# Output projection of a transformer block: three of the eight pairs of K tiles in its second half as seven products

## The chip, the cores and the metric

The kernel runs on one core of a Trainium2 chip. TensorE (in the profile: PE for its matmuls, PEld for its weight loads) multiplies and writes to PSUM, which has eight banks of 128 x 512 float32. VectorE (DVE) and ScalarE (ACT) do elementwise work, GpSimd (POOL) a few small steps, and SyncE (SP) issues nearly all loads from memory. The metric is the time of one run on the device in microseconds (us), less being better. Each engine takes its instructions in the order in which the program writes them; engines wait for each other through semaphores.

## The reference, cut to what matters

One layer of a hybrid encoder, on 256 tokens of width 2048, all in float32: an input projection, eight heads of retention and eight of latent attention, an output projection, a layer norm, a feed-forward part of width 8192, and a second layer norm.

```python
def reference(x, positions, w_in, ..., w_out, ln1_g, ln1_b, w_up, w_down, ln2_g, ln2_b):
    ...
    mix = jnp.concatenate([ret_out, mla_out], axis=-1) @ w_out[l]      # (256, 2048) @ (2048, 2048)
    x = _layer_norm(DEEPNORM_ALPHA * x + mix, ln1_g[l], ln1_b[l])
    h = jnp.square(jax.nn.relu(x @ w_up[l])) @ w_down[l]
    x = _layer_norm(DEEPNORM_ALPHA * x + h, ln2_g[l], ln2_b[l])
    return x
```

## The kernel before, in words

**Split operands.** Every matmul operand `a` is held as two tiles of TensorE's rounded type: `hi`, a cast by ScalarE, and `lo = a - hi`, a subtraction by VectorE. A product is three matmuls: hi with hi, hi with lo, lo with hi. The activations of the output projection are `mix`: 16 K tiles of 128 rows, each with 256 columns of hi (one per token) and 256 of lo.

**Weights as jobs.** Weights arrive as a list of jobs (`weights`, L174 to L205; `weights_pair` for the feed-forward part). A job has a load of 1 MB into one of three raw tiles (tag `raw`) and pieces that split the raw tile, 1024 columns each: a cast (L190) and a subtraction (L191). The hi and lo tiles come from a ring of five slots (`NSLOT`). `next_piece` (L135) issues the next piece of the list; a piece that needs a slot goes out only if the matmuls of the piece five before it have been issued (`free` marks that). `unit` (L209) is called after each group of matmuls: it advances every generator in the list `side` by one step, and then issues up to two pieces. So side work and weight pieces get their places in the engines' instruction streams by the order of these calls. A job with `held` set stops the list until it is cleared. The last three pairs of the output projection's second half do not use slots: their pieces (`staged_out`) go to tiles of their own, `wsx` and `wst`.

**The output projection** (L821 to L841) computes two halves of 1024 columns. A half is eight steps; each takes a pair of K tiles, `kp = (i + 4) % 8`, so the heads of latent attention come first. For each of the two row blocks `tb` of 128 tokens a step issues 12 matmuls of 128 x 512 (two K tiles, three each, two PSUM banks; `xstat`, L302), and after them a `unit`. A half has four banks, `ao[tb][j]`, of the tag `acc`; the second half reuses those of the first. In the last step of the first half, `residual` (L813) adds each finished bank to the scaled residual stream `xt` (L818) and takes its statistics (L819); block 0's two residuals stand ahead of the `unit` after block 0's matmuls, block 1's ahead of the next.

The second half runs its first five steps in that loop. Its last three, staged, are issued bank by bank (`out_bank`, L916) with the first layer norm between them: `out_bank(0, 0)`, its residual, a `unit`, `out_bank(0, 1)`, its residual, `stats` of block 0, four `n_norm` (L869), five sixths of `out_bank(1, 0)`, and then `n_trans` (L875, tiles `x1t`), the transposes of the first normalised columns, into PSUM banks of the second tag, `wk`. TensorE has this order too.

**Seven products.** The up and down projections of the feed-forward part already do some pairs of K tiles by a Strassen-like scheme (`seven_products`, matmuls at L1090). The pair's weights are a 2 x 2 block matrix, and so are its activations (two K tiles by two row blocks). Seven products instead of eight, 21 matmuls instead of 24, use sums of weight blocks (`weight_sums`, L400 to L402, three VectorE operations) and sums of activation blocks (`token_sums`, L364 to L369). Such a pair has three and a half splits where a plain pair has two. Four of the products collect in four extra banks, which are added to the results afterwards (`add_sums`, L1176, in the down projection).

Of the kernel before, what the change touches and what calls it, by code (L numbers as in the profile page):

```python
# [8 lines left out]
F32 = mybir.dt.float32  # L9
# [5 lines left out]
P = 128  # L15
D = 2048
S = 256
# [22 lines left out]
STORED = (12, 9, 22, 25, 4, 7)  # L40


UP_PAIRS = (3, 5, 6)
UP_SEVEN = ((), (3, 5)) + 6 * (UP_PAIRS,)
NHELD = 4
# [35 lines left out]
def kernel(  # L81
# [35 lines left out]
    def bank(name):  # L117
        return psum.tile([P, 512], F32, tag="wk", name=name)
# [43 lines left out]
    def raw_tile(job, name):  # L162
        job.raw = wraw.tile([P, 2048], F32, tag="raw", name=name)
        return job.raw

    def weights(src, n, name, into=None, width=1024, cuts=None):

        job = Job(None, [], into is None)
        job.width = width
        spans = list(zip(cuts, cuts[1:])) if cuts else [(0, n)]  # L170

        def load():
            raw = raw_tile(job, f"raw_{name}")
            for i, (a, b) in enumerate(spans):  # L174
                (nc.scalar if name == "mla0" and i == 0 else nc.sync).dma_start(raw[:, a:b], src[:, a:b])

        def piece(i):
            a, m = i * width, min(width, n - i * width)
            if into is None:
                hi = wsp.tile([P, 1024], F32R, tag="hi", name=f"hi_{name}_{i}")  # L180
                lo = wsp.tile([P, 1024], F32R, tag="lo", name=f"lo_{name}_{i}")
            else:
                hi, lo = into(i)
            job.hi.append(hi)
            job.lo.append(lo)
            for o, e in spans if cuts else ((a, a + m),):
                o, e = max(o, a) - a, min(e, a + m) - a
                if o < e:
                    r = job.raw[:, a + o:a + e]
                    nc.scalar.copy(hi[:, o:e], r)  # L190
                    nc.vector.tensor_sub(lo[:, o:e], r, hi[:, o:e].bitcast(F32))  # L191

        job.load = load
        job.pieces = [lambda i=i: piece(i) for i in range((n + width - 1) // width)]
        job.free = [[False] for _ in job.pieces]
        jobs.append(job)
        return job

    def other(load, pieces):
        job = Job(None, pieces, False)  # L200
        job.load = lambda: load(job)
        job.free = []
        jobs.append(job)
        return job
# [121 lines left out]
    def staged_out(i):  # L326
        def into(j):
            if i == 0:
                t = work.tile([P, 2048], F32R, tag="big", name=f"wsx{j}", bufs=2)
                return t[:, 0:1024], t[:, 1024:2048]  # L330
            if "out" not in staged:
                staged["out"] = slab.tile([P, 8192], F32R, tag="slab", name="wst")
            o = (2 * i - 2 + j) * 2048
            return staged["out"][:, o:o + 1024], staged["out"][:, o + 1024:o + 2048]
        return into

    for half in range(2):
        row = []
        for i in range(KT // 2):
            kp = (i + H // 2) % (KT // 2)  # L340
            n = i - (KT // 2 - 3)
            row.append(weights(w_out[half, kp], 2048, f"wo{half}{kp}",
                               into=staged_out(n) if half and n >= 0 else None))
        j_out.append(row)
    norm_rows = {}

    def row_job(i, pieces):
        def load(job):
            norm_rows[i] = raw_tile(job, f"row{i}")
            nc.sync.dma_start(norm_rows[i], ln_rows[i:i + 1].partition_broadcast(P))  # L350
        other(load, pieces)

    def x1_piece(i, tb, a):
        c = xt[:, tb, a:a + 1024]
        op = nc.vector.tensor_mul if i == 0 else nc.vector.tensor_add
        op(c, c, norm_rows[i][:, a:a + 1024])


    extra = {}

    def token_sums(r0, r1, st, v):
# [9 lines left out]
    def weights_pair(name, load, half, columns, sums=None, seven=False, into=None):  # L371
# [44 lines left out]
        jobs.append(job)  # L416
        return job

    def up_pair(b, kp):
        def load(job):  # L420
            raw = raw_tile(job, f"raw_wu{b}_{kp}")
            nc.sync.dma_start(raw.rearrange("p (f c) -> p f c", f=8),
                              w_up[8 * b:8 * b + 8, :, kp * 256:(kp + 1) * 256].rearrange("f p c -> p f c"))

        def half(job, e, i, j):
            return job.raw.rearrange("p (f e c) -> p f e c", f=8, e=2)[:, i:j, e]

        def columns(job, t):
            v = job.raw.rearrange("p (f e c) -> p f e c", f=8, e=2)
            return (v[:, 4:8].rearrange("p f e c -> p e f c"), v[:, :, 0].rearrange("p (j f) c -> p j f c", j=2),  # L430
                    t.rearrange("p (j f c) -> p j f c", j=2, c=P))

        return weights_pair(f"wu{b}_{kp}", load, half, columns, None, kp in UP_SEVEN[b])

    def down_pair(p, pair, into=None, seven=None):
# [16 lines left out]
                    job.raw[:, 0:1024].rearrange("p (j c) -> p j c", j=2), t.rearrange("p (j c) -> p j c", j=2))  # L452

        return weights_pair(f"wd{p}_{pair}", load, half, columns, None if seven is None or p == 1 and pair in STORED else sums, seven is not None, into)

    def sums_view(t):
        return t.rearrange("p (i h c) -> p i h c", i=4, h=2)

    def sums_of(q, pair):
        q = 2 + STORED.index(pair) if pair in STORED else q  # L460
# [352 lines left out]
    def residual(tb, j, pb, st, scaled=False):  # L813
# [4 lines left out]
            nc.vector.scalar_tensor_tensor(c, c, ALPHA, pb, op0=ALU.mult, op1=ALU.add)  # L818
        nc.vector.bn_stats(st[:, j], c)  # L819

    def out_steps(half, i):  # L821
        kp = (i + H // 2) % (KT // 2)
        hi, lo = use(j_out[half][i])
        return [(mix, 2 * kp + j, hi, lo, j * 1024) for j in range(2)]

    for half in range(2):
        ao = [[acc(f"o{half}{tb}{j}") for j in range(2)] for tb in range(2)]
        for i in range(KT // 2 - 3 * half):
            if half == 1 and i == 0:
                assert not side  # L830
                work_cm.__exit__(None, None, None)
                work = ctx.enter_context(tc.tile_pool(name="work2", bufs=1))
            steps = out_steps(half, i)
            for tb in range(2):
                xstat(ao[tb], steps, (512, 512), i == 0, half == 0 and i == KT // 2 - 1, tb)
                if half == 0 and i == KT // 2 - 1:
                    for j in range(2):
                        residual(tb, j, ao[tb][j], st1[tb])
                if tb == 1:
                    free(j_out[half][i])  # L840
                unit()  # L841

    mvs, rss = [None] * 2, [None] * 2

# [7 lines left out]
    w_staged = []  # L852
    for i in range(3):
        w_staged += out_steps(1, KT // 2 - 3 + i)
    x1hl = slab.tile([P, KT, 512], F32R, tag="slab", name="x1hl")
    pts = {}


# [58 lines left out]
        xstat(ao[tb], w_staged[part], (512, 512), False, last, tb, banks=(j,))  # L917

    out_bank(0, 0)
    residual(0, 2, ao[0][0], st1[0])  # L920
    unit()
    out_bank(0, 1)
    residual(0, 3, ao[0][1], st1[0])
    stats(0, st1[0])
    unit(1)
    q4 = [range(4 * q, 4 * q + 4) for q in range(4)]
# [7 lines left out]
    n_hi(0, q4[0])  # L934
    n_trans(0, q4[1])
    n_trans(0, q4[2])
    residual(1, 2, ao[1][0], st1[1])
    n_affine(0, q4[1], False)
    n_affine(0, q4[2], True)
    n_lo(0, q4[0])  # L940
# [6 lines left out]
    n_lo(0, q4[2])  # L947
    n_hi(0, q4[3])
    out_bank(1, 1, slice(2, 6), True)
    residual(1, 3, ao[1][1], st1[1])  # L950
    stats(1, st1[1])
    for q in range(2):
        up_half(0, q4[q])
# [113 lines left out]
    def pair_products(job, x, k, cb, first, last, done=None):  # L1067
        for e in range(2):
            hi, lo = use(job, e + 1)
            for tb in range(2):  # L1070
                xstat(cb[tb], [(x, k + e, hi, lo, e * 1024)], (512, 512), first and e == 0, last and e == 1, tb)
                if tb == 1:
                    free(job, (e,))
                elif done and e == 1:
                    side.append(done)
                unit()

    def seven_products(job, x, k, sums, cb, mb, first, last):
        for a, w, o, pb, alone in ((("x", 1, 0), 0, 0, cb[0][0], False), (("s", 3), 0, 512, cb[0][1], False),
                                   (("x", 0, 0), 1, 0, mb[0], True), (("s", 1), 1, 512, mb[1], True),  # L1080
                                   (("s", 0), 2, 0, mb[2], True), (("s", 2), 2, 512, mb[3], True),
                                   (("x", 1, 1), 3, 0, cb[1][0], False)):
            use(job, w + 1)
            if a[0] == "x":
                h, l = (x[:, k + a[1], i * S + a[2] * P:i * S + (a[2] + 1) * P] for i in range(2))
            else:
                h, l = (sums[:, a[1], i] for i in range(2))
            hi, lo = job.hi[w][:, o:o + 512], job.lo[w][:, o:o + 512]
            for x_part, w_part, fst, lst in ((h, hi, True, False), (h, lo, False, False), (l, hi, False, True)):
                nc.tensor.matmul(pb, x_part, w_part, start=alone and first and fst, stop=alone and last and lst)  # L1090
            if o or w == 3:
                free(job, (w,))
                unit()

    def up_gather(mb):
# [293 lines left out]
```

## Time and profile before

| | |
|---|---|
| median of 3 runs | 1112.53 us (1112.09 to 1113.03) |
| span of the profiled execution, first to last instruction | 1110.6 us |
| TensorE busy | 1102.9 us, 99% of the span |
| VectorE busy | 901.0 us, 81% |
| ScalarE busy | 613.8 us, 55% |
| first matmul of the output projection | at 320.0 us |
| its last matmul (`out_bank(1, 1)`) ends | at 413.2 us |

The profiled execution's own time is its span with what lies around it; the median stands 1.93 us above the span. Times within the program are microseconds from the start of the span. In rows of the timeline and of the chain, the first number is the start and the second the length; `L` is the line of the kernel, `out<-in` the tiles, `x` the number of instructions, and a bracket tells how long the engine was idle before and what ended it.

### The profile page before, as it was taken

To read this page: it belongs to the slowest core of one execution; us is meant where nothing else is said; L and a number is where in the kernel's file an instruction comes from. 1 tells how busy PE (TensorE), PEld (TensorE's weight loads), DVE (VectorE), ACT (ScalarE), POOL (GpSimd) and SP (SyncE) were. 2 spreads that over 40 slices of the span, in tenths; PEclk is the share of its full clock that TensorE was granted. 3 is DMA by queue.
4 is the path that set the end of the run, shared out by engine and by line. 5 is a ranking of instruction groups with operands and counts; after the bars stand their busy time and mean duration, and the time that the engine had idled before them with its cause. 6 is when DMAs were issued, how large, how long until landed. Compare 5 with 4: busy or idle time off the path is not lost.

```text
span 1110.6 us, 13644 instructions
## 1 busy us (share of the span) xinstructions
PE 1102.9 (99%) x5193; PEld 921.7 (83%) x5193; DVE 901.0 (81%) x1198; ACT 613.8 (55%) x793; POOL 9.6 (1%) x18
## 2 busy tenths in 40 slices
PE   9999999999999999999999999999999999999997
PEld 8888888888888889888888888888888888888885
DVE  6676684666656777898998999899999998999886
ACT  4445664535453446455656656656666673665650
POOL 0000000000000000000000000000000000000000
PEclk9999999999999999999999999999999999999999
DMA  8655365444465554566656756755656665656672
GB/s 306 222 205 192 119 228 184 145 168 161 144 258 197 199 198 152 189 216 207 222 166 213 221 158 193 221 168 180 223 191 195 204 213 196 215 189 200 204 251 104
DMA packets 92561, 217.08 MB, mean 195 GB/s; under 512 B 4177, under 2 KB 62545, under 8 KB 84433
## 3 DMA queue, kind: packets, MB, share of 16 engines
q1 hardware_dynamic: 92064, 215.64, 57.7%
q8 instruction: 40, 0.66, 0.2%
q10 hardware_dynamic: 432, 0.59, 0.2%
q14 instruction: 25, 0.20, 0.1%
HBM read 214.12 MB, written 2.10 MB: 195 GB/s over the span
## 4 chain that ended last, share of the span: by engine, by line
PE 96%; DVE 2%; DMA 1%; issue 0%; ACT 0%; POOL 0%; DVEq 0%; ACTq 0%; POOLq 0%
PE d L302 20%; PE u L302 18%; PE r L302 16%; PE o L302 8%; PE v L1090 5%; PE m L302 5%; PE s L1090 4%; PE u L1090 4%; PE d L1090 3%; PE up L734 2%; PE pu L734 2%; PE ut L1137 1%; PE pv L302 1%; PE up L740 1%; PE pu L740 1%; PE pq L302 1%
## 5 line engine op out<-in xcount | busy, mean ns | idle before, releaser
L302 PE MATMUL d<-hi_wd,rhl 128*128 128x512 f32 x664 | 182.9, 390 | 0.0
L389 ACT CAST hi_wu<-raw_wu 128x1024 fp32r<-128x1024 f32 x112 | 118.1, 1058 | 116.6 <-DVE raw_wu L401 57.9
L389 ACT CAST hi_wd<-raw_wd 128x1024 fp32r<-128x1024 f32 x125 | 130.0, 1052 | 75.8 <-PE d L302 33.5
L390 DVE TENSOR_TENSOR lo_wd<-raw_wd,hi_wd 128x1024 fp32r<-128x1024 f32 x125 | 148.6, 1220 | 18.2 <-ACT hi_wd L389 17.4
L302 PE MATMUL u<-hi_wu,x1hl 128*128 128x512 f32 x576 | 162.7, 393 | 0.0
L390 DVE TENSOR_TENSOR lo_wu<-raw_wu,hi_wu 128x1024 fp32r<-128x1024 f32 x112 | 133.3, 1220 | 23.4 <-ACT hi_wu L389 22.6
L302 PE MATMUL r<-hi_ret,xhl 128*128 128x512 f32 x512 | 147.1, 397 | 0.0
L302 PEld LDWEIGHTS d<-hi_wd,rhl 128*128 128x128 f32 x664 | 124.3, 188 | 25.7
L302 PEld LDWEIGHTS u<-hi_wu,x1hl 128*128 128x128 f32 x576 | 106.4, 188 | 20.9
L302 PEld LDWEIGHTS r<-hi_ret,xhl 128*128 128x128 f32 x512 | 93.9, 188 | 18.2
L302 PE MATMUL d<-lo_wd,rhl 128*128 128x512 f32 x332 | 102.6, 389 | 0.1
L191 DVE TENSOR_TENSOR lo_ret<-raw_ret,hi_ret 128x1024 fp32r<-128x1024 f32 x64 | 75.7, 1220 | 23.9 <-ACT hi_ret L190 23.7
L302 PE MATMUL u<-lo_wu,x1hl 128*128 128x512 f32 x288 | 88.9, 390 | 0.0
L302 PE MATMUL r<-lo_ret,xhl 128*128 128x512 f32 x256 | 79.4, 391 | 0.0
L190 ACT CAST hi_ret<-raw_ret 128x1024 fp32r<-128x1024 f32 x64 | 64.9, 1051 | 16.4 <-PE r L302 12.2
L302 PEld LDWEIGHTS d<-lo_wd,rhl 128*128 128x128 f32 x332 | 62.2, 188 | 13.4 <-DVE lo_wd L390 0.6
L302 PEld LDWEIGHTS u<-lo_wu,x1hl 128*128 128x128 f32 x288 | 54.1, 188 | 11.4
L302 PE MATMUL o<-hi_wo,mix 128*128 128x512 f32 x208 | 57.1, 392 | 0.0
L302 PEld LDWEIGHTS r<-lo_ret,xhl 128*128 128x128 f32 x256 | 48.1, 188 | 10.4
L191 DVE TENSOR_TENSOR lo_wo<-raw_wo,hi_wo 128x1024 fp32r<-128x1024 f32 x26 | 31.2, 1222 | 19.6 <-ACT hi_wo L190 18.9
L302 PEld LDWEIGHTS o<-hi_wo,mix 128*128 128x128 f32 x208 | 38.7, 188 | 7.8
L302 PE MATMUL m<-hi_mla,xhl 128*128 128x512 f32 (+1 forms) x168 | 42.5, 363 | 0.0
(297 smaller groups left out, 1908.6 us busy)
## 6 DMA issues: line engine op xcount, KB each, us to landing
raw_wu<-in_w_up SPq DMA_DIRECT2D x64, 1024.0 KB, 5.7
raw_wd<-in_w_down SPq DMA_DIRECT2D x64, 1024.0 KB, 5.5
raw_ret<-in_w_ret SPq DMA_DIRECT2D x32, 1024.0 KB, 4.8
raw_wo<-in_w_out SPq DMA_DIRECT2D x16, 1024.0 KB, 4.8
raw_mla<-in_w_mla SPq DMA_DIRECT2D x14, 672.0 KB, 4.7
raw_qk<-in_w_qk SPq DMA_DIRECT2D x8, 640.0 KB, 3.9
row<-in_ln_rows SPq DMA_DIRECT2D x4, 1024.0 KB, 4.7
raw_uv<-in_w_uv SPq DMA_DIRECT2D x2, 1024.0 KB, 4.7
```

The source lines that it names most:

```text
L190: nc.scalar.copy(hi[:, o:e], r)
L191: nc.vector.tensor_sub(lo[:, o:e], r, hi[:, o:e].bitcast(F32))
L302: nc.tensor.matmul(accs[j][:, :w], x_part, w_part[:, a:a + w], start=first and fst and i == 0, stop=last and lst and i == len(steps) - 1)
L389: nc.scalar.copy(h, src)
L390: nc.vector.tensor_sub(l, src, h.bitcast(F32))
L734: nc.tensor.matmul(pb, hi[:, a:a + P], hl[:, k0 + i], start=first and i == ks[0], stop=last and i == ks[-1])
L740: nc.tensor.matmul(pb[:, 0:S], lo[:, a:a + P], hl[:, k0 + i, 0:S], start=False, stop=last and i == ks[-1])
L1090: nc.tensor.matmul(pb, x_part, w_part, start=alone and first and fst, stop=alone and last and lst)
L1137: nc.tensor.transpose(pts[i][:, f * P:(f + 1) * P], gathered[i][:, f * P:(f + 1) * P], ident)
```

## The change

Three pairs of the second half, steps 1, 2 and 3, become seven-product pairs (`out_pair`). Their sums of activations (`out_token_sums`) are a generator that enters `side` at step 3 of the first half; they are kept in the still unused tile `x1hl`, which for that is allocated earlier. The scratch tiles for sums of weights (`t13`, `t4`) and the four extra banks (`mb`) are allocated at the last step of the first half, where the pool `work` is replaced; until then the first of the three jobs is `held`. The four extra banks are evacuated by `add_out`, a generator of four steps that runs during step 4, which has two `unit` calls after each block in place of one. Since `add_out` scales the residual stream, the four residuals of the second half add without scaling. `seven_products` and `sums_view` are moved, unchanged.

```diff
+OUT_SEVEN = (1, 2, 3)
+SUMS_AT = 3
+WORK2 = (0, 7)
...
+    def out_pair(half_, kp):
+        def load(job):
+            nc.sync.dma_start(raw_tile(job, f"raw_wo{half_}{kp}"), w_out[half_, kp])
...
+        return weights_pair(f"wo{half_}_{kp}", load, half, columns, None, True)
+
+    def out_token_sums(q):
+        k = 2 * ((OUT_SEVEN[q] + H // 2) % (KT // 2))
+        k = slice(k, k + 2)
+        xs = spare_flat[:, 0:512].rearrange("p (k t) -> p k t", k=2)
+        nc.vector.tensor_add(xs, mix[:, k, 0:S].bitcast(F32), mix[:, k, S:].bitcast(F32))
+        st = spare_flat[:, 512:].rearrange("p (i c) -> p i c", i=4)
+        rest = token_sums(xs[:, 0], xs[:, 1], st, out_sums(q))
+        yield
+        rest()
+        yield
...
-            row.append(weights(w_out[half, kp], 2048, f"wo{half}{kp}",
-                               into=staged_out(n) if half and n >= 0 else None))
+            if half == 1 and i in OUT_SEVEN:
+                row.append(out_pair(half, kp))
+            else:
+                row.append(weights(w_out[half, kp], 2048, f"wo{half}{kp}",
+                                   into=staged_out(n) if half and n >= 0 else None))
+    j_out[1][OUT_SEVEN[0]].held = True
...
+    def add_out(mb):
+
+        p1, p6, p5, p7 = mb
+        u, v = spare_flat[:, 0:512], spare_flat[:, 512:]
+
+        def plus(j, tb, src):
+            c = xt[:, tb, (2 + j) * 512:(3 + j) * 512]
+            nc.vector.scalar_tensor_tensor(c, c, ALPHA, src, op0=ALU.mult, op1=ALU.add)
+
+        nc.scalar.copy(u, p1)
+        plus(0, 0, p1)
+        yield
+        nc.vector.tensor_add(u, u, p6)
+        nc.vector.tensor_add(v, u, p5)
+        yield
+        plus(1, 0, v)
+        nc.vector.tensor_add(u, u, p7)
+        yield
+        plus(0, 1, u)
+        nc.vector.tensor_add(u, u, p5)
+        plus(1, 1, u)
+
+    x1hl = slab.tile([P, KT, 512], F32R, tag="slab", name="x1hl")
+
+    def sums_ahead():
+        for q in range(len(OUT_SEVEN)):
+            yield from out_token_sums(q)
+
     for half in range(2):
         ao = [[acc(f"o{half}{tb}{j}") for j in range(2)] for tb in range(2)]
         for i in range(KT // 2 - 3 * half):
-            if half == 1 and i == 0:
+            if half == 0 and i == SUMS_AT:
+                side.append(sums_ahead())
+            if half == WORK2[0] and i == WORK2[1]:
                 assert not side
                 work_cm.__exit__(None, None, None)
                 work = ctx.enter_context(tc.tile_pool(name="work2", bufs=1))
+                extra["t13"] = work.tile([P, 1024], F32, tag="xf", name="ot13")
+                extra["t4"] = work.tile([P, 512], F32, tag="ut", name="ot4")
+                mb = [bank(f"os{j}") for j in range(4)]
+                j_out[1][OUT_SEVEN[0]].held = False
+            if half == 1 and i in OUT_SEVEN:
+                q = OUT_SEVEN.index(i)
+                seven_products(j_out[1][i], mix, 2 * ((i + H // 2) % (KT // 2)), out_sums(q), ao, mb,
+                               q == 0, i == OUT_SEVEN[-1])
+                if i == OUT_SEVEN[-1]:
+                    side.append(add_out(mb))
+                continue
             steps = out_steps(half, i)
             for tb in range(2):
                 xstat(ao[tb], steps, (512, 512), i == 0, half == 0 and i == KT // 2 - 1, tb)
...
                 unit()
+                if half == 1 and i > OUT_SEVEN[-1]:
+                    unit()
...
-    residual(0, 2, ao[0][0], st1[0])
+    residual(0, 2, ao[0][0], st1[0], True)
...
-    residual(0, 3, ao[0][1], st1[0])
+    residual(0, 3, ao[0][1], st1[0], True)
...
-    residual(1, 2, ao[1][0], st1[1])
+    residual(1, 2, ao[1][0], st1[1], True)
...
-    residual(1, 3, ao[1][1], st1[1])
+    residual(1, 3, ao[1][1], st1[1], True)
```

More of the change, by code (lines that the diff above doesn't have):

```diff
@@ L335, in staged_out @@
         return into
[L337 to L341, printed above, removed]
-            row.append(weights(w_out[half, kp], 2048, f"wo{half}{kp}",
-                               into=staged_out(n) if half and n >= 0 else None))
[L344 to L356, printed above, removed]
     extra = {}
@@ L417, in weights_pair, with sums_view, half, columns @@
         return job
+    def sums_view(t):
+        return t.rearrange("p (i h c) -> p i h c", i=4, h=2)
+    def out_pair(half_, kp):
+        def load(job):
+            nc.sync.dma_start(raw_tile(job, f"raw_wo{half_}{kp}"), w_out[half_, kp])
+        def half(job, e, i, j):
+            return job.raw[:, e * 1024 + i * P:e * 1024 + j * P]
+        def columns(job, t):
+            return (job.raw.rearrange("p (e j c) -> p e j c", e=2, j=2)[:, :, 1],
+                    job.raw[:, 0:1024].rearrange("p (j c) -> p j c", j=2), t.rearrange("p (j c) -> p j c", j=2))
+        return weights_pair(f"wo{half_}_{kp}", load, half, columns, None, True)
[9 more added lines that the diff above has]
+        yield
+    def out_sums(q):
+        return sums_view(x1hl[:, 2 * q:2 * q + 2].rearrange("p k t -> p (k t)"))
+    for half in range(2):
+        row = []
+        for i in range(KT // 2):
+            kp = (i + H // 2) % (KT // 2)
+            n = i - (KT // 2 - 3)
+            if half == 1 and i in OUT_SEVEN:
[3 more added lines that the diff above has]
+                                   into=staged_out(n) if half and n >= 0 else None))
+        j_out.append(row)
+    j_out[1][OUT_SEVEN[0]].held = True
+    norm_rows = {}
+    def row_job(i, pieces):
+        def load(job):
+            norm_rows[i] = raw_tile(job, f"row{i}")
+            nc.sync.dma_start(norm_rows[i], ln_rows[i:i + 1].partition_broadcast(P))
+        other(load, pieces)
+    def x1_piece(i, tb, a):
+        c = xt[:, tb, a:a + 1024]
+        op = nc.vector.tensor_mul if i == 0 else nc.vector.tensor_add
+        op(c, c, norm_rows[i][:, a:a + 1024])
     def up_pair(b, kp):
@@ L454, in down_pair @@
         return weights_pair(f"wd{p}_{pair}", load, half, columns, None if seven is None or p == 1 and pair in STORED else sums, seven is not None, into)
-    def sums_view(t):
-        return t.rearrange("p (i h c) -> p i h c", i=4, h=2)
     def sums_of(q, pair):
@@ L819, in residual, with seven_products @@
         nc.vector.bn_stats(st[:, j], c)
+    def seven_products(job, x, k, sums, cb, mb, first, last):
+        for a, w, o, pb, alone in ((("x", 1, 0), 0, 0, cb[0][0], False), (("s", 3), 0, 512, cb[0][1], False),
+                                   (("x", 0, 0), 1, 0, mb[0], True), (("s", 1), 1, 512, mb[1], True),
+                                   (("s", 0), 2, 0, mb[2], True), (("s", 2), 2, 512, mb[3], True),
+                                   (("x", 1, 1), 3, 0, cb[1][0], False)):
+            use(job, w + 1)
+            if a[0] == "x":
+                h, l = (x[:, k + a[1], i * S + a[2] * P:i * S + (a[2] + 1) * P] for i in range(2))
+            else:
+                h, l = (sums[:, a[1], i] for i in range(2))
+            hi, lo = job.hi[w][:, o:o + 512], job.lo[w][:, o:o + 512]
+            for x_part, w_part, fst, lst in ((h, hi, True, False), (h, lo, False, False), (l, hi, False, True)):
+                nc.tensor.matmul(pb, x_part, w_part, start=alone and first and fst, stop=alone and last and lst)
+            if o or w == 3:
+                free(job, (w,))
+                unit()
     def out_steps(half, i):
@@ L841 @@
                 unit()
+                if half == 1 and i > OUT_SEVEN[-1]:
+                    unit()
+    assert not side
     mvs, rss = [None] * 2, [None] * 2
@@ L854 @@
         w_staged += out_steps(1, KT // 2 - 3 + i)
-    x1hl = slab.tile([P, KT, 512], F32R, tag="slab", name="x1hl")
     pts = {}
@@ L1075, in pair_products @@
                     side.append(done)
[L1076 to L1092, printed above, removed]
                 unit()
```

## The prediction

> **What bounds the kernel now.** I read the page first, for the busy shares.
>
> ```profile
> span 1110.6 us, 13644 instructions
> ## 1 busy us (share of the span) xinstructions
> PE 1102.9 (99%) x5193; PEld 921.7 (83%) x5193; DVE 901.0 (81%) x1198; ACT 613.8 (55%) x793; POOL 9.6 (1%) x18
> ```
>
> TensorE never rests; VectorE rests a fifth of the time. Next, the chain that ended last, around a pair in the up projection that is already done as seven products, then around the end of the output projection (columns: start, us, what).
>
> ```profile
> 477.51 1.36 PE u L1090 x6
> 478.87 2.72 PE v L1090 x12
> 481.59 0.68 PE u L1090 x3
> 482.27 5.44 PE u L302 x24
> ```
>
> ```profile
> 359.93 46.70 PE o L302 x206
> 406.62 0.46 PE x1t L875 x4
> ...
> 410.46 2.77 PE o L302 x12
> ```
>
> A seven-product pair is 21 matmuls in 1.36 + 2.72 + 0.68 = 4.76 us, a plain pair 24 in 5.44 us. The second fence shows that in the output projection only TensorE is on the path, up to x1t, the first transposes of the normalised rows. These are the first matmuls there that need a result of VectorE. So I read VectorE from the end of the first half to that point: the busy table (PE, PEld, DVE, ACT, POOL busy; clock; DMA) and the timeline (start, us; in brackets the idle time before and what ended it).
>
> ```profile
> 320.00:362.23 42.23, 42.23 (x201) 35.27 (x200) 24.03 (x39) 20.01 (x23) 1.01 (x1) 1.00 0.62 230
> 364.95:405.82 40.87, 40.87 (x182) 33.84 (x181) 29.63 (x32) 18.24 (x18) 0.55 (x1) 1.00 0.68 254
> ```
>
> ```profile
> 362.23 2.54 DVE L191 TENSOR_TENSOR lo_wo<-raw_wo,hi_wo 128x1024 fp32r<-128x1024 f32 x2 [2.86 <-ACT hi_wo L190]
> 364.95 0.69 DVE L818 SCALAR_TENSOR_TENSOR xm<-xm,o 128x512 f32<-128x512 f32 x1 [0.18 <-PE o L302]
> ...
> 370.32 2.34 DVE L191 TENSOR_TENSOR lo_wo<-raw_wo,hi_wo 128x1024 fp32r<-128x1024 f32 x2
> 373.06 2.58 DVE L191 TENSOR_TENSOR lo_wo<-raw_wo,hi_wo 128x1024 fp32r<-128x1024 f32 x2 [0.40 <-ACT hi_wo L190]
> 378.50 2.59 DVE L191 TENSOR_TENSOR lo_wo<-raw_wo,hi_wo 128x1024 fp32r<-128x1024 f32 x2 [2.85 <-ACT hi_wo L190]
> 383.94 1.23 DVE L191 TENSOR_TENSOR lo_wo<-raw_wo,hi_wo 128x1024 fp32r<-128x1024 f32 x1 [2.85 <-ACT hi_wo L190]
> 385.08 2.36 DVE L191 TENSOR_TENSOR wsx<-raw_wo,wsx 128x1024 fp32r<-128x1024 f32 x2
> ...
> 391.09 2.36 DVE L191 TENSOR_TENSOR wst<-raw_wo,wst 128x1024 fp32r<-128x1024 f32 x2 [1.38 <-ACT wst L190]
> 394.10 2.36 DVE L191 TENSOR_TENSOR lo_wu<-raw_wu,hi_wu 128x1024 fp32r<-128x1024 f32 x2 [0.65 <-ACT hi_wu L190]
> 396.80 1.22 DVE L191 TENSOR_TENSOR lo_wu<-raw_wu,hi_wu 128x1024 fp32r<-128x1024 f32 x1 [0.34 <-ACT hi_wu L190]
> 399.18 0.69 DVE L818 SCALAR_TENSOR_TENSOR xm<-xm,o 128x512 f32<-128x512 f32 x1 [1.16 <-PE o L302]
> ...
> 400.51 2.34 DVE L191 TENSOR_TENSOR lo_wu<-raw_wu,hi_wu 128x1024 fp32r<-128x1024 f32 x2
> 403.26 0.69 DVE L818 SCALAR_TENSOR_TENSOR xm<-xm,o 128x512 f32<-128x512 f32 x1 [0.40 <-PE o L302]
> ...
> 405.82 0.55 DVE L869 TENSOR_SCALAR xm<-xm,lnmv,lnrs 128x512 f32<-128x512 f32 x1 [0.66 <-POOL lnrs L278]
> ```
>
> From 364.95, where VectorE takes up the first half's residuals, to 405.82, where it starts to normalise, its order is the program's. The bracketed idle before the last row is 0.40 + 2.85 + 2.85 + 1.38 + 0.65 + 0.34 + 1.16 + 0.40 = 10.03 us; that is all the room in the 40.87 us. The last 0.66 us is a wait for POOL that stays. The norm's first piece ends near 406.4, and the transposes follow at once: room at that point is about 0.1 us.
>
> **The change, part by part.** *Matmuls.* Three pairs at 4.76 instead of 5.44 us: 9 matmuls, 3 x 0.68 = 2.04 us less on TensorE.
>
> *VectorE, per pair.* These are rows of two seven-product pairs in a row in the up projection:
>
> ```profile
> 568.55 1.22 DVE L400 TENSOR_TENSOR t<-raw_wu 128x1024 f32<-128x1024 f32 x1
> 569.81 0.69 DVE L401 TENSOR_TENSOR raw_wu<-raw_wu,t 128x512 f32<-128x512 f32 x1
> 570.53 0.69 DVE L402 TENSOR_TENSOR ut<-raw_wu 128x512 f32<-128x512 f32 x1
> 571.14 2.35 DVE L390 TENSOR_TENSOR lo_wu<-raw_wu,hi_wu 128x1024 fp32r<-128x1024 f32 x2
> ...
> 575.15 1.22 DVE L400 TENSOR_TENSOR t<-raw_wu 128x1024 f32<-128x1024 f32 x1
> ```
>
> One seven-product pair occupies VectorE from 568.55 to 575.15, 6.60 us: 2.59 for the sums of weights, 4.01 for three and a half splits. A plain pair's two splits take 2.36. Three pairs add 3 x 4.24 = 12.72 us.
>
> *VectorE, evacuation.* `add_out` issues 8 operations of 128x512 (and one ScalarE copy). The rows nearest are those of `add_sums`, with the sums of activations of the up projection in the same view of groups (busy, mean ns):
>
> ```profile
> L369 DVE TENSOR_TENSOR us<-xm,us 128x512 fp32r<-128x512 f32 x3 | 2.1, 684 | 0.0
> L1058 DVE TENSOR_TENSOR xm<-x1hl 128x512 f32<-128x512 f32 x3 | 2.1, 684 | 0.0
> ...
> L1187 DVE TENSOR_TENSOR xm<-xm,s 128x512 f32<-128x512 f32 x2 | 1.4, 680 | 0.0
> ...
> L364 DVE TENSOR_TENSOR xm<-xm 128x128 f32<-128x128 f32 x3 | 0.9, 291 | 0.1
> ```
>
> 8 x 0.68 = 5.44 us. The four later residuals become plain adds: 0.68 for 0.69, nothing. `add_out` hands its PSUM banks back ahead of the residuals in VectorE's order, so the banks add no wait of their own.
>
> *The hold.* `held` on the first such pair keeps its pieces out until the last pair of the first half. One split done today at 362.23 (the second of that row) moves behind 364.95: 1.18 us. No transfer is added; SP's later loads follow later splits and are counted as waits below.
>
> *Order.* The pieces of the first pair (sums of weights, one split: 2.59 + 1.18 = 3.8 us) now stand between the first half's residuals of row block 0 and of block 1, for the slots that they need are free by then (today none is). Block 1's banks, which the second half overwrites, come free 3.8 us later.
>
> ```profile
> 394.90 1.52 PE L302 MATMUL o<-wsx,mix 128*128 128x512 f32 x6
> ```
>
> The second half's five pairs end at 394.90, so it begins at 394.90 - 5 x 5.44 = 367.7, and TensorE wants block 1's banks half a pair later, at 370.4. VectorE gets there at 364.95 + 2.7 (block 0: half of 364.95 to 370.32) + 3.8 = 371.4 and is through both banks three operations of 0.69 later, at 373.5: a new wait of 3.1 us. It is not added to the sum, since VectorE is further behind at the end.
>
> *Sums of activations.* Per pair 0.68 + 4 x 0.29 + 0.68 = 2.5 us of VectorE, 7.6 for three, issued between 336 and 362. There VectorE is busy 24.03 of 42.23 us, so 18.2 are free; each consumer is two steps off. I take 0. Without that cover it could cost up to 7.6.
>
> *ScalarE.* Three times one and a half casts (2.00 us for two, below) plus five copies: under 9 us against 22.6 free. Nothing.
>
> ```profile
> 390.00 2.00 ACT L190 CAST wst<-raw_wo 128x1024 fp32r<-128x1024 f32 x2 [2.29 <-DMA raw_wo<-in_w_out]
> ```
>
> *Sum on VectorE.* Added before the norm: 12.72 + 5.44 + 1.18 = 19.34 us. Of the 10.03 us of room, the 1.38 and 0.65 stay: they are a chain of split, reload of that buffer, cast, split, and VectorE's list between those splits is unchanged (four splits, then the staged one). So 8.0 us are filled. Two double rows (2.58, 2.59 against 2.34) hide another 0.49. The norm is 19.34 - 8.0 - 0.49 = 10.85 us later, 10.7 after the 0.1 of room. If those waits vanish too it is 8.7; if the 0.49 cannot be used, 11.3. TensorE's 2.04 us does not enter: it only arrives earlier at a wait. The list behind the norm is unchanged, and nothing there can give the delay back, because TensorE has no idle to absorb it.
>
> TensorE meets the delay as three waits, together 10.7 + 2.04 = 12.7 us. The first is the 3.1 at the banks: the second half's first pair ends at 373.5 + 2.6 = 376.1, the next two at 385.6. The third seven-product pair's first split is done at 364.95 + 5.37 (residuals) + 2 x 6.60 + 3.77 = 387.3: a wait of 1.8. The rest, 7.8 us, falls in one piece ahead of x1t.
>
> *The clock.* What does TensorE do after 7.8 idle us? The nearest rows are at the program's end:
>
> ```profile
> 1104.92 1.02 PE L1293 MATMUL last<-row,warm 128*128 128x512 f32 x2
> ...
> 1108.00:1110.60 2.60, 0.00 (x0) 0.00 (x0) 0.00 (x0) 0.00 (x0) 0.00 (x0) 0.71 0.36 123
> ```
>
> TensorE stops at 1105.94, and in the last 2.60 us the granted clock averages 0.71. If it went to half, it did so 0.29 x 2.60 / 0.5 = 1.5 us before the end, at 1109.1: about 3.2 us after the last matmul. So 7.8 idle us should bring it down; the waits of 3.1 and 1.8 should not. No row shows how fast it returns. Between nothing and half clock for all work from 406.46 to 413.23 (6.8 us lost), I take a return as long as the fall: 3.2 us at half speed, 1.6 us lost, all on the path, since TensorE leads there.
>
> [...]
>
> Sum: 10.7 + 1.6 = 12.3 us. The profiled span of 1110.6 becomes 1122.9. The median of the runs, 1112.53, stands 1.93 above the span (what lies around it), so 1124.8.
>
> **The rivals.** *The clock holds.* The same backlog, no slow stretch: 1112.53 + 10.7 = 1123.2. For it: nothing shows the clock at a restart, and the first wait may split the idle time otherwise than I have it. Against: the 0.71.
>
> *Part of the backlog slips behind the norm.* If the up weights' two splits that precede the second residual (2.34) or the last step of `add_out` (three operations, 2.0) came after it, the norm would be 2.3 to 4.4 us earlier, 1119 to 1122. Against: pieces leave by freed slots, in the program's order, and two more steps now come before the residuals, not fewer.
>
> *VectorE keeps up* (the other side). Place: the norm's start. It decides if the work added before it stays under the 10 us of room. Then 2.04 us are won: 1110.5. For it: the quoted back-to-back pairs, after which the up projection's matmuls follow on without a gap. Against: there no result waits for VectorE's end and plain pairs follow; here 6.60 us per pair meet 4.76 of matmuls three times, then evacuation and staged splits. A pair would have to add 1.1 us, not 4.24.
>
> **How the numbers follow.** About 0.2% (2.2 us) is what a measurement of this kernel tells from no change; even the full 2.04 us is inside it. Chances: forecast 0.55 (own range 1122 to 1128), clock holds 0.23, part slips 0.08, VectorE keeps up 0.10 (0.07 within 0.2%, 0.03 beyond it), a clock that stays low for much longer or unhidden sums of activations 0.04 (up to 1131). The range 1119.5 to 1128 leaves out the last two and a little of the slip. Slower 0.90, same 0.07, faster 0.03.
>
> **What would show it.** Right: VectorE without idle from 365 to about 416; a TensorE wait for the residuals near 370; one of some 8 us ahead of x1t, ended by VectorE; granted clock well under 1 for some us behind it; 9 matmuls fewer; no change in length of any stage after. Wrong: x1t starting before 410, or VectorE idle in the second half.

## The result, and the profile after

| | before | after |
|---|---|---|
| median of the runs of this comparison | 1112.76 us | 1125.24 us (1123.4 to 1125.67) |
| ratio, 95% interval | 1 | 1.011 (1.0097 to 1.0123) |
| span of the profiled execution | 1110.6 us | 1123.9 us |
| first layer norm starts (VectorE) | 405.82 | 416.91 |
| first transposes x1t start (TensorE) | 406.46 | 417.51 |

The kernel is 12.5 us slower. The page's first lines of the changed kernel:

```profile
span 1123.9 us, 13681 instructions
## 1 busy us (share of the span) xinstructions
PE 1102.6 (98%) x5184; PEld 919.9 (82%) x5184; DVE 924.0 (82%) x1239; ACT 620.4 (55%) x803; POOL 9.9 (1%) x18
```

TensorE issues 9 matmuls fewer (5184 for 5193) and VectorE is busy 23 us longer. VectorE's timeline from the first half's last residuals to the norm:

```profile
365.01 0.69 DVE L852 SCALAR_TENSOR_TENSOR xm<-xm,o 128x512 f32<-128x512 f32 x1 [0.26 <-PE o L305]
...
367.66 1.21 DVE L381 TENSOR_TENSOR ot<-raw_wo 128x1024 f32<-128x1024 f32 x1
...
371.37 0.68 DVE L852 SCALAR_TENSOR_TENSOR xm<-xm,o 128x512 f32<-128x512 f32 x1
...
398.45 2.36 DVE L194 TENSOR_TENSOR wst<-raw_wo,wst 128x1024 fp32r<-128x1024 f32 x2 [1.49 <-ACT wst L193]
401.94 1.23 DVE L194 TENSOR_TENSOR lo_wu<-raw_wu,hi_wu 128x1024 fp32r<-128x1024 f32 x1 [1.13 <-ACT hi_wu L193]
403.08 0.68 DVE L884 SCALAR_TENSOR_TENSOR xm<-xm,os 128x512 f32<-128x512 f32 x1
...
412.43 0.69 DVE L884 SCALAR_TENSOR_TENSOR xm<-xm 128x512 f32<-128x512 f32 x1
413.04 0.68 DVE L850 TENSOR_TENSOR xm<-xm,o 128x512 f32<-128x512 f32 x1
...
416.91 1.91 DVE L963 TENSOR_SCALAR xm<-xm,lnmv,lnrs 128x512 f32<-128x512 f32 x4 [0.67 <-POOL lnrs L281]
```

From 365.01 to 416.91 VectorE waits only at three places: 1.49 and 1.13 us for reloaded weights, 0.67 us for POOL. The sums of weights (L381) stand ahead of block 1's residual (371.37). The evacuation (L884) and the up weights stand ahead of the second half's first residual, which runs at 413.04, though its bank was finished near 402. TensorE's timeline, after and then before, where it meets this:

```profile
372.11 0.50 PE L305 MATMUL o<-hi_wo,mix 128*128 128x512 f32 x1 [1.47 <-DVE xm L852]
373.42 0.50 PE L305 MATMUL o<-hi_wo,mix 128*128 128x512 f32 x1 [0.81 <-DVE xm L852]
...
387.33 0.50 PE L867 MATMUL o<-lo_wo,mix 128*128 128x512 f32 x1 [1.37 <-DVE lo_wo L371]
...
417.51 1.12 PE L969 MATMUL x1t<-ident,xm 128*128 128x128 f32 x4 [8.29 <-DVE xm L963]
...
428.71 0.76 PE L969 MATMUL x1t<-ident,xm 128*128 128x128 f32 x4 [0.21 <-DVE xm L963]
```

```profile
406.46 0.63 PE L875 MATMUL x1t<-ident,xm 128*128 128x128 f32 x4
...
416.29 0.76 PE L875 MATMUL x1t<-ident,xm 128*128 128x128 f32 x4 [0.21 <-DVE xm L869]
```

There are three waits, and x1t starts 11.05 us later. From block 0's x1t to block 1's it takes 11.20 us after and 9.83 before, for the same work: another 1.37 us. The busy table of the changed kernel shows why (the value ahead of the DMA share is the granted clock):

```profile
411.00:413.00 2.00, 0.00 (x0) 0.00 (x0) 1.93 (x4) 0.00 (x0) 0.00 (x0) 1.00 0.75 295
413.00:415.00 2.00, 0.00 (x0) 0.00 (x0) 1.97 (x4) 0.00 (x0) 0.00 (x0) 0.63 0.48 201
415.00:417.00 2.00, 0.00 (x0) 0.00 (x0) 1.23 (x5) 0.00 (x0) 0.55 (x1) 0.50 0.00 0
417.00:419.00 2.00, 1.49 (x6) 1.40 (x7) 1.82 (x4) 0.34 (x1) 0.00 (x0) 0.50 0.00 0
419.00:421.00 2.00, 2.00 (x12) 1.70 (x11) 1.02 (x2) 1.79 (x5) 0.00 (x0) 0.66 0.00 0
421.00:423.00 2.00, 2.00 (x13) 1.65 (x12) 2.00 (x6) 1.85 (x5) 0.00 (x0) 1.00 0.00 0
```

The clock is at half from about 413.5 to 420.4, so the first 2.8 us of work run at half speed. 11.05 + 1.37 = 12.42 us, which is the change of the medians (12.48). This one execution is 13.3 us longer in span; the 0.9 us on top stand near 1064, where the chain that ended last holds one load of down weights of 6.54 us after and 5.66 us before, in code that the change does not touch.

### The profile page after: what moved, and what is told of

It is laid out like the page before. It is cut to its first block, busy times and chain, and to the rows that moved or that the text cites. A ratio compares the mean times of both kernels' runs of the same rounds, so it can differ in the third digit from the quotient of the medians.

```text
span 1123.9 us, 13681 instructions
## 1 busy us (share of the span) xinstructions
PE 1102.6 (98%) x5184; PEld 919.9 (82%) x5184; DVE 924.0 (82%) x1239; ACT 620.4 (55%) x803; POOL 9.9 (1%) x18
## 4 chain that ended last, share of the span: by engine, by line
PE 91%; DVE 6%; DMA 2%; issue 1%; ACT 1%; POOL 0%; SPq 0%; DVEq 0%; ACTq 0%
PE d L305 20%; PE u L305 17%; PE r L305 16%; PE v L867 5%; PE m L305 4%; PE s L867 4%; PE o L305 4%; PE u L867 4%; PE d L867 3%; PE up L768 2%; PE pu L768 2%; PE ut L1214 1%; PE pv L305 1%; DVE lo_wo L371 1%; PE up L774 1%; DMA raw_mla<-in_w_mla 1%
## 5 line engine op out<-in xcount | busy, mean ns | idle before, releaser
L305 PE MATMUL o<-hi_wo,mix 128*128 128x512 f32 x160 | 45.0, 394 | 2.3 <-DVE xm L852 2.3
L867 PE MATMUL v<-hi_wu,us 128*128 128x512 f32 x120 | 40.2, 389 | 0.0
L194 DVE TENSOR_TENSOR lo_mla<-raw_mla,hi_mla 128x320 fp32r<-128x320 f32 (+2 forms) x34 | 26.7, 814 | 14.1 <-ACT hi_mla L193 13.8
```

The lines of the kernel that those rows point to most:

```text
L305: nc.tensor.matmul(accs[j][:, :w], x_part, w_part[:, a:a + w], start=first and fst and i == 0, stop=last and lst and i == len(steps) - 1)
```

## Experiments

Theory A, from the prediction: VectorE's work ahead of the first norm is compared with its idle time there, and the excess delays the norm. Rival B: each seven-product pair brings TensorE its own wait, in proportion. Rival C: the loss begins where the first pair's sums of weights come between the residuals. After the first four runs theory A was replaced by A2, below.

All results in one table. "Up" is the start of the first split of up weights, "tail" the time from it to the norm, "x1t wait" TensorE's idle time ahead of the transposes, "stretch" the time from block 0's x1t to block 1's.

| kernel | median us | ratio (interval) | up | norm | tail | x1t wait | stretch |
|---|---|---|---|---|---|---|---|
| before | 1112.3 to 1112.8 | 1 | 394.10 | 405.82 | 11.72 | 0 | 9.83 |
| the change | 1125.24 | 1.0110 (1.0097 to 1.0123) | 401.94 | 416.91 | 14.97 | 8.29 | 11.20 |
| e1, step 3 alone | 1121.27 | 1.0076 (1.0064 to 1.0089) | 397.91 | 412.75 | 14.84 | 7.36 | 12.45 |
| e2, steps 2 and 3 | 1119.77 | 1.0061 (1.0046 to 1.0077) | 397.20 | 412.05 | 14.85 | 7.34 | 12.29 |
| e3, hold later | 1125.21 | 1.0113 (1.0099 to 1.0127) | 401.41 | 417.38 | 15.97 | 8.50 | 11.48 |
| e4, busy wait | 1123.22 | 1.0095 (1.0082 to 1.0109) | 400.72 | 416.60 | 15.88 | 1.18 | 9.89 |
| e5, 24 matmuls | 1124.92 | 1.0109 (1.0094 to 1.0124) | 401.14 | 416.06 | 14.92 | 5.75 | 12.40 |
| e6, two splits | 1117.59 | 1.0044 (1.0027 to 1.0061) | 393.82 | 409.20 | 15.38 | 4.82 | 11.52 |
| e7, GpSimd | 1129.96 | 1.0151 (1.0136 to 1.0166) | – | 420.54 | – | 7.26 | 12.57 |
| e8, no evacuation | 1122.97 | 1.0092 (1.0077 to 1.0107) | 400.58 | 413.47 | 12.89 | 5.39 | 11.99 |
| e9, step 1 alone | 1117.31 | 1.0040 (1.0027 to 1.0054) | 400.56 | 410.60 | 10.04 | 0.23 | 9.89 |
| e10, step 1, hold later | 1114.08 | 1.0019 (1.0010 to 1.0028) | 396.69 | 407.39 | 10.70 | 1.80 | 9.88 |

**e1 and e2: one pair, two pairs.**

```diff
-OUT_SEVEN = (1, 2, 3)
+OUT_SEVEN = (3,)
```

This is the edit of e1; e2 has `(2, 3)` in its place.

> Only step 3 of the second half is a seven-product pair. Theory A (VectorE's total work ahead of the first layer norm against its idle time there): added work 4.24 + 5.44 = 9.7 us (nothing is held back early), 8.5 us of it fill idle time, so the norm starts about 1.2 us later than at 405.8 and the time is about 1113.7 us (1112 to 1115.5); TensorE waits once, under 3 us, and its clock stays at 1.00. Rival B (every seven-product pair costs TensorE its own wait, in proportion): a third of 12.5 us, 1116.9 us. Rival C (the loss starts with the early order, the sums of weights between the two blocks' residuals): no such order here, so 0.68 us is won, 1112.1 us.

> Steps 2 and 3 are seven-product pairs. Theory A: added 2 x 4.24 + 5.44 = 13.9 us against 8.5 us of idle time, so the norm is 5.4 us later; the wait ahead of the transposes is 5 to 7 us and the clock falls, which costs 1 to 2.5 us more: 1119.5 us (1117.5 to 1121). Rival B (in proportion to the pairs): 8.3 us, 1121 us, with the waits spread over the pairs. Rival C (early order): no wait for the residuals' banks, 1111.4 us.

e2's time lies in A's range, though its norm is 6.2 us late where A said 5.4; e1 missed all three theories, and one pair cost no less than two (the intervals of the two ratios overlap). VectorE's timeline of e1, and behind it ScalarE's, whose casts VectorE waits for:

```profile
383.61 0.69 DVE L371 TENSOR_TENSOR lo_wo<-ot,hi_wo 128x512 fp32r<-128x512 f32 x1 [2.41 <-ACT hi_wo L370]
385.40 2.54 DVE L194 TENSOR_TENSOR lo_wo<-raw_wo,hi_wo 128x1024 fp32r<-128x1024 f32 x2 [1.10 <-ACT hi_wo L193]
...
397.91 1.22 DVE L194 TENSOR_TENSOR lo_wu<-raw_wu,hi_wu 128x1024 fp32r<-128x1024 f32 x1 [1.56 <-ACT hi_wu L193]
...
412.75 1.46 DVE L963 TENSOR_SCALAR xm<-xm,lnmv,lnrs 128x512 f32<-128x512 f32 x3 [0.66 <-POOL lnrs L281]
```

```profile
382.95 0.62 ACT L370 CAST hi_wo<-ot 128x512 fp32r<-128x512 f32 x1 [3.01 <-PE o L305]
384.31 1.05 ACT L193 CAST hi_wo<-raw_wo 128x1024 fp32r<-128x1024 f32 x1 [0.74 <-PE o L305]
...
396.83 1.05 ACT L193 CAST hi_wu<-raw_wu 128x1024 fp32r<-128x1024 f32 x1 [1.93 <-DMA raw_wu<-in_w_up]
```

Two things follow. First, the idle time cannot all be filled: the pair takes four of the five slots, its last split and those of the plain pair behind it wait for slots (2.41 and 1.10 us, for casts that wait for TensorE's matmuls to free the slot), and the reloads behind them (loads into a raw tile that has to be split first) push the first up split from 394.10 to 397.91. Second, the evacuation stands behind that split, where VectorE's list had only 1.9 us of idle time left: the tail grows from 11.72 to 14.84 us. 3.81 + 3.12 = 6.93 us, the whole delay of the norm. This is theory A2: the norm's start is the start of the first up split, set by VectorE's backlog or by slots and reloads, plus a tail which is solid once the evacuation stands in it. TensorE's long wait then costs the clock in addition (granted: 0.50 from 409 to 417 in e1 and from 408 to 416 in e2): the stretch is 2.6 us longer in e1 and 2.5 in e2, against 1.4 in the changed kernel, which is why their times do not follow the norm alone.

**e3: the hold ends later.**

```diff
-                j_out[1][OUT_SEVEN[0]].held = False
...
+                if half == 0 and i == KT // 2 - 1 and tb == 1:
+                    j_out[1][OUT_SEVEN[0]].held = False
```

> As the changed kernel, but the first seven-product pair is held until both blocks' residuals of the first half are issued. Theory A: TensorE no longer waits for the two banks near 370 (2.3 us go), but VectorE's list ahead of the norm is the same, so the norm starts near 416.9 as before, the wait ahead of the transposes grows by what is saved, and the time stays, 1125 us (1123.5 to 1126.5). Rival C (the early order costs): 2.3 us and more are won, 1122.5 us.

As theory A said: the wait at the banks is gone, other waits grow, and the time stays. They do not grow where it was expected, though: the wait ahead of the transposes is 8.50 us, hardly longer than 8.29, and the rest is now spent on waits for the three pairs' splits (0.64, 1.54 and 1.54 us). Rival C fails for three pairs.

**e4: TensorE kept busy during its wait.**

```diff
     out_bank(1, 0, slice(0, 5), False)
+    idle = bank("idle")
+    for i in range(32):
+        nc.tensor.matmul(idle, mix[:, 0, 0:P], w_staged[0][2][:, 0:512], start=True, stop=True)
     n_trans(0, q4[0])
```

> As the changed kernel, with 32 further matmuls of 128x512, into a bank that nobody reads, placed ahead of the first transposes, where TensorE idles for 8.3 us. Theory (the idle time lowers the clock, which costs 1.4 us of matmuls afterwards): the granted clock stays 1.00 from 405 to 425, the norm starts at 416.9 as before, and the time falls by 1.4 us, to 1123.8 us (1123.2 to 1124.2). Rival (matmuls behind the wait are slow for another reason, or VectorE leads there): no change, 1125.2 us.

The granted clock stays at 1.00 behind the wait (409 to 423 in the table below) and the stretch goes back to 9.89 us (9.83 before). The time falls by 2.0 us against the changed kernel's median, a little more than the 1.4 of the one profiled execution, and within the 1.4 to 2.7 us by which the stretch was longer in the other kernels that wait. So the slow matmuls behind the wait come from the wait, and from nothing else in the change. Its busy table:

```profile
372.00:374.00 2.00, 1.19 (x5) 0.80 (x5) 1.97 (x4) 0.00 (x0) 0.00 (x0) 0.92 0.00 0
374.00:376.00 2.00, 2.00 (x6) 1.55 (x5) 2.00 (x3) 0.62 (x1) 0.00 (x0) 0.50 0.22 33
376.00:378.00 2.00, 2.00 (x8) 1.60 (x7) 1.97 (x3) 0.53 (x1) 0.00 (x0) 0.72 0.82 307
409.00:417.00 8.00, 7.02 (x31) 5.47 (x30) 7.13 (x12) 0.19 (x1) 0.55 (x1) 1.00 0.39 135
417.00:423.00 6.00, 5.80 (x34) 4.98 (x35) 5.76 (x13) 5.07 (x13) 0.00 (x0) 1.00 0.01 3
```

**e5: 24 matmuls again.**

```diff
+            if x is mix and w == 3:
+                for x_part, w_part in ((h, hi), (h, lo), (l, hi)):
+                    nc.tensor.matmul(pb, x_part, w_part, start=False, stop=False)
```

> As the changed kernel, but each of the three pairs issues 24 matmuls (the last product is repeated), so TensorE has the 2.04 us of matmuls again while VectorE's list is unchanged. Theory (the norm's start, set by VectorE, decides): the norm starts at 416.9 as before, the wait ahead of the transposes is shorter by what the matmuls add, and the time stays: 1125.2 us (1124 to 1126). Rival (TensorE's matmuls still count): 2 us more, 1127.3 us.

2.04 us of matmuls come back and the time does not move (1124.92 and 1125.24, intervals nearly equal). In the profiled executions two smaller things cancel: x1t starts 0.84 us earlier than in the changed kernel (416.67 for 417.51), since VectorE waits less for reloads there (1.18 and 0.68 us for 1.49 and 1.13), and the stretch behind it is 1.20 us longer, since more of the work runs slowly: six matmuls that follow the x1t there (wsx, from 420.42) take 2.37 us, and 1.63 in the changed kernel (from 420.81). The saving that the change is made of is swallowed by the wait for VectorE.

**e6: without the sums of weights and the further splits.**

```diff
+        if name[:2] == "wo":
+            def second():
+                split(1, half(job, 0, 0, 8))
+                for t in (job.hi, job.lo):
+                    t += [t[0], t[1]]
+            job.pieces = [lambda: split(0, half(job, 1, 0, 8)), second]
+            job.loose = 0
...
-            use(job, w + 1)
+            use(job, min(w + 1, len(job.free)))
...
```

> As the changed kernel, but the three pairs' jobs leave out the sums of weights and the third and fourth split (the products use the two remaining pieces), so VectorE and ScalarE do for these pairs what they do for plain ones; 21 matmuls each and the evacuation of the four extra banks stay. Theory A (total work against total idle): 6.6 us added against 8.5 us of idle time, the norm is not late, and TensorE's saving shows: 1111 us. Theory A2, from the run with one pair (the list that follows the arrival of the first up weights, five splits, the evacuation and the two residuals, is solid and 15.2 us long instead of 11.7, and its start hangs on the reloads): the norm starts 2 to 4 us late, at 408 to 410, TensorE waits about 5 us, and the clock may fall: 1116.5 us (1114.5 to 1118.5). Rival (the matmul order of the seven products costs): 1120 us or more.

A2 had it, A did not. VectorE's timeline of e6:

```profile
393.82 2.36 DVE L194 TENSOR_TENSOR lo_wu<-raw_wu,hi_wu 128x1024 fp32r<-128x1024 f32 x2 [0.59 <-ACT hi_wu L193]
...
409.20 1.92 DVE L975 TENSOR_SCALAR xm<-xm,lnmv,lnrs 128x512 f32<-128x512 f32 x4 [0.66 <-POOL lnrs L281]
```

The first up split is back in its old place (393.82; in the kernel before, 394.10): of the 6.6 us added only the 1.18 of the hold stand ahead of it. The 5.44 us of the evacuation stand in the tail, where 1.9 us were idle, and make the norm 3.4 us late; the slower stretch behind TensorE's wait (11.52 us for 9.83) adds 1.7.

**e8: without the evacuation.**

```diff
-                if i == OUT_SEVEN[-1]:
-                    side.append(add_out(mb))
```

> As the changed kernel, but the evacuation of the four extra banks (eight operations of VectorE, one of ScalarE) is left out; the sums of weights and all splits stay. Theory A and A2: VectorE is late by its splits until the first up weights (402 instead of 394), and 5.4 us shorter behind: the norm starts at 411.5 to 412.5, the wait ahead of the transposes is about 3 us, and the time is 1119.5 us (1118 to 1122, the upper part if the clock falls). If the evacuation alone were the cause: 1111 to 1113 us.

The cause is shared, as expected, but the norm comes 1 us later than the upper end that I gave, and the time is 1 us above it. The tail still takes 12.89 us, more than the 11.72 of the kernel before:

```profile
404.20 2.36 DVE L194 TENSOR_TENSOR lo_wu<-raw_wu,hi_wu 128x1024 fp32r<-128x1024 f32 x2 [1.26 <-ACT hi_wu L193]
408.45 1.22 DVE L194 TENSOR_TENSOR lo_wu<-raw_wu,hi_wu 128x1024 fp32r<-128x1024 f32 x1 [1.89 <-ACT hi_wu L193]
```

Without the evacuation between them the up splits wait for their reloads, 1.26 and 1.89 us. Of its 5.4 us only 3.4 were net.

**e7: sums of weights and up subtractions on GpSimd.**

```diff
-                    nc.vector.tensor_sub(lo[:, o:e], r, hi[:, o:e].bitcast(F32))
+                    eng = nc.gpsimd if name in ("wu0", "wu1", "wu2") else nc.vector
+                    eng.tensor_tensor(lo[:, o:e], r, hi[:, o:e].bitcast(F32), op=ALU.subtract)
...
-            nc.vector.tensor_sub(t13, second, first)
...
+            eng = nc.gpsimd if name[:2] == "wo" else nc.vector
+            eng.tensor_tensor(t13, second, first, op=ALU.subtract)
...
```

> As the changed kernel, but the three operations of each sum of weights and the subtractions of the first three up weights (six splits) run on GpSimd, which is idle here; that takes 7.8 + 5.9 us off VectorE's list ahead of the norm. Theory A2: what VectorE keeps fits, the norm starts at 405.5 to 407.5, and the time is 1110.5 to 1113 us if GpSimd needs no more than twice VectorE's time and does not slow VectorE. Rival (GpSimd is much slower on these, or holds VectorE up): the splits behind the sums come later than now, 1118 us or more.

The rival was right: 17 us slower than before. GpSimd's groups, one row of its timeline, and then VectorE's timeline while GpSimd works:

```profile
L195 POOL TENSOR_TENSOR lo_wu<-raw_wu,hi_wu 128x1024 fp32r<-128x1024 f32 x6 | 15.5, 2610 | 23.9 <-ACT hi_wu L193 23.9
L383 POOL TENSOR_TENSOR ot<-raw_wo 128x1024 f32<-128x1024 f32 x3 | 8.6, 2866 | 25.8 <-DMA raw_wo<-in_w_out 15.9 <-DVE lo_wo L372 9.9
```

```profile
385.49 2.77 POOL L383 TENSOR_TENSOR ot<-raw_wo 128x1024 f32<-128x1024 f32 x1 [2.30 <-DVE lo_wo L372]
```

```profile
362.40 5.66 DVE L195 TENSOR_TENSOR lo_wo<-raw_wo,hi_wo 128x1024 fp32r<-128x1024 f32 x2
...
385.93 3.41 DVE L372 TENSOR_TENSOR lo_wo<-raw_wo,hi_wo 128x1024 fp32r<-128x1024 f32 x1
```

Beside VectorE, GpSimd takes 2.6 to 2.9 us for what takes VectorE 1.2. VectorE's own subtractions stretch too while GpSimd runs: one takes 3.4 us, and two together take 5.7 where they take 2.4 otherwise. The one of 3.4 us starts at 385.93, 0.44 us after an operation of GpSimd, and ends at 389.34, 1.08 us after the end of that operation at 388.26; the same subtraction at 370.61, where GpSimd is idle, takes 1.21 us. How one engine holds the other up the rows do not show.

**e9 and e10: one pair, at step 1; e10 with the later hold of e3.**

```diff
-OUT_SEVEN = (1, 2, 3)
+OUT_SEVEN = (1,)
```

> Only step 1 of the second half is a seven-product pair, so its evacuation runs in step 2, where VectorE has idle time, and two plain pairs follow before the staged ones. The matmuls and VectorE operations are those of the run with step 3 alone. Theory A2 (what counts is the solid list behind the first up weights, and when these arrive): the list behind them is 11.7 us again, and what is left is the excess of total work, 4.24 + 5.44 + 1.18 = 10.9 us against 8.5 us of idle time: the norm starts about 2.4 us late, TensorE waits 2.3 us for the residuals' banks and about 1 us at the transposes, the clock stays, and the time is 1114.5 us (1112.5 to 1116), clearly under the 1121.3 us of step 3 alone. Rival (one pair and its evacuation cost the same wherever they stand): 1121 us.

> As the run with step 1 alone, but the pair is held until both blocks' residuals of the first half are issued. Theory A2: no wait for the residuals' banks; the norm starts 2.4 us late as there, the only wait is about 3 us at the transposes, near the limit at which the clock falls: 1114.9 us (1113.5 to 1117). If the wait for the banks was what set the time of the run with step 1 alone: 1112 us, level with the kernel before.

The operations of e1, two steps earlier: 4.0 us faster in e9, 7.2 in e10. Position counts, as A2 says: the tail is 10.0 and 10.7 us, not 14.8. e10 lies in its range. e9 is 1.3 us above its own, and its norm is 4.8 us late instead of 2.4. VectorE idles there for a split whose cast waits for matmuls, and these run at half clock (VectorE, TensorE's matmuls, and the busy table of e9):

```profile
379.33 1.23 DVE L194 TENSOR_TENSOR lo_wo<-raw_wo,hi_wo 128x1024 fp32r<-128x1024 f32 x1 [1.88 <-ACT hi_wo L193]
```

```profile
376.26 1.05 PE L305 MATMUL o<-lo_wo,mix 128*128 128x512 f32 x2
```

```profile
374.00:376.00 2.00, 2.00 (x7) 1.60 (x8) 2.00 (x3) 0.31 (x1) 0.00 (x0) 0.73 0.00 0
376.00:378.00 2.00, 2.00 (x7) 1.51 (x6) 1.45 (x2) 0.31 (x1) 0.00 (x0) 0.50 0.62 143
378.00:380.00 2.00, 2.00 (x10) 1.63 (x9) 0.67 (x1) 1.34 (x2) 0.00 (x0) 0.92 0.90 381
```

Behind the two waits at the banks (2.3 us in all, the longer 1.5) the clock was at half from about 374.9 to 378.3, and TensorE had work all that time: 3.4 us at half speed are 1.7 us lost, which is nearly all of VectorE's 1.88. The runs agree: the one run of e9 with a mean clock of 1.000 took 1115.38 us, inside the range, and the other four, at 0.998, took 1117.24 to 1117.89. So rival C has a point here, mostly by way of the clock.

The early order costs nothing where VectorE is solid behind it (e3). Between e9 and e10 the medians differ by 3.2 us; the slow clock explains 1.7 to 1.9 of them, and the rest stays open. No variant beat the kernel before; the nearest, e10, is 0.19% (0.10 to 0.28%) slower.

## Why the prediction was right, point by point

- **VectorE's sum.** Said: the norm 10.85 us later. Measured: 11.09. A pair took 6.6 us, as in the up projection. The two reload waits stayed, slightly longer (1.49 and 1.13 for 1.38 and 0.65).
- **The saving does not enter.** Shown by e5, in the time; its norm did not stay exactly in place.
- **The waits.** Said: 3.1, 1.8 and 7.8 us. Measured as idle time: 1.47 + 0.81, 1.37 and 8.29, at the three places named. The prediction calls the transposes the first matmuls that need a result of VectorE; the lo weights are such results too, and the 1.37 us is a wait for one.
- **The early order.** Said: not added to the sum. Shown by e3 for three pairs; e9 shows that it holds only where VectorE stays solid, so that neither the wait at the banks nor the slow clock behind it matters.
- **The clock.** Said: 1.6 us. Measured: 1.37 in the profiled execution, about 2.0 between e4 and the change. That the size fits so well is partly luck: half clock was assumed there (the rows before showed a mean of 0.71; those of the changed kernel show 0.50), the time to the return was a guess, and in the kernels that wait 4.8 us or more ahead of the transposes the stretch is anything from 1.4 to 2.7 us longer. The limit of about 3 us that the prediction and e10's expectation count with was the author's estimate from the program's end, and no run shows one: the clock stayed at 1.00 in e10 with a wait of 1.80 us, and fell in e4 and e9 behind two of 1.5 and 0.8 us. The guess that the short waits near 370 leave the clock alone held in the profiled execution of the changed kernel (1.00 from 364 to 413) and failed in those of e4 and e9, where it was at half for 3.4 us behind the same two waits. In e4 VectorE sets the start of the norm anyway; in e9 it cost 1.7 us.
- **Sums of activations.** Said: 0. The first half's last residuals begin at 365.01; in the kernel before, at 364.95.
- **What was wrong.** The point from which "VectorE keeps up" was to decide, 10 us of added work: e6 adds 6.6 us and e1 9.7, and the norm is 3.4 and 6.9 us late. By the prediction a pair that adds 1.1 us of VectorE breaks even; in e6 a pair's splits add nothing, and the kernel is still 5 us slower. The idle time was counted as one pool, while most of it lies ahead of the evacuation and some of it cannot be reached for want of slots. With three pairs VectorE is solid up to the reload waits, and the sum came out all the same.
- **Still open.** What share of e1's loss by slots would go with a sixth slot was not tried.

## What to carry to other kernels

Before shaving matmuls off a stage, find the first point behind it where TensorE waits for the engine that does the extra work, and sum that engine's list up to it, in order: idle time ahead of the added work does not help, and idle time held by buffers cannot be used. A long wait of TensorE cost twice here, once as idle time and once as slow matmuls behind it. Behind every wait of 4.8 us or more ahead of the transposes the stretch took 11.20 to 12.57 us for 9.83, and the granted clock there was 0.50 in the change, e1, e2 and e3. Two waits of 1.5 and 0.8 us close together had a clock of 0.50 behind them in e4 and e9 and of 1.00 in the changed kernel; one of 1.8 us ahead of the transposes (e10) left it at 1.00. The same work placed two steps earlier cost 4 to 7 us less here, and handing part of it to an idle engine made it worse (e7, 4.7 us above the change).

## What the runs showed of the hardware that was not expected

The low stretches of the clock had few different lengths. From the rows above it is at half for about 6.8 us in the changed kernel (413.5 to 420.4) and 3.4 us in e4 (373.7 to 377.1) and e9 (374.9 to 378.3). The table of e1 gives about 10.2 us (408.6 to 418.8):

```profile
407.00:409.00 2.00, 0.00 (x0) 0.00 (x0) 1.93 (x4) 0.00 (x0) 0.00 (x0) 0.89 0.71 291
...
417.00:419.00 2.00, 2.00 (x8) 1.67 (x7) 2.00 (x6) 1.51 (x5) 0.00 (x0) 0.55 0.00 0
```

The tables of e2 and, behind it, e3 give 10.2 us (407.6 to 417.8) and 6.8 us (414.6 to 421.4):

```profile
406.00:408.00 2.00, 0.00 (x0) 0.00 (x0) 1.93 (x4) 0.00 (x0) 0.00 (x0) 0.90 0.94 279
...
416.00:418.00 2.00, 2.00 (x8) 1.71 (x7) 2.00 (x6) 1.21 (x4) 0.00 (x0) 0.54 0.00 0
```

```profile
414.00:416.00 2.00, 0.00 (x0) 0.00 (x0) 1.93 (x4) 0.00 (x0) 0.00 (x0) 0.66 0.31 127
...
420.00:422.00 2.00, 2.00 (x11) 1.79 (x10) 1.55 (x3) 1.39 (x4) 0.00 (x0) 0.64 0.00 0
```

These six stretches are one, two and three times 3.4 us. The falls do not follow the waits at a fixed distance: the clock fell 2.6 us after TensorE had stopped in e1 (405.99) and 4.3 us after in the changed kernel (409.22), and in e4 it fell after two waits of 1.5 and 0.8 us with matmuls between them. What sets the lengths and the moment of the fall is not shown by these runs.
